# Second mixer of a two-layer trunk: the joins of the block inverses in four parts each, and operands of three post steps requested one step ahead

## Chip, cores, metric

One Trainium2 chip, one core. The metric is the time of one execution in device microseconds (us); lower is better. All data are float32.

## What is computed

Two layers of a streaming encoder run on 1104 tokens side by side: 16 learned tokens and 1024 prompt tokens of one request, and 64 tokens of another that brings its own state. Layer 0 is a gated delta-rule mixer with an MLP, layer 1 the mixer that the change is in (RWKV-7) with an MLP. Cut to layer 1's mixer, for the normalised input h (D = 1024, 16 heads of 64):

```python
xx = shift(h) - h
xr, xw, xk, xv, xa, xg = h + xx * mu          # six mixes
r, k, v = xr @ w_r, xk @ w_k, xv @ w_v
w_log = -softplus(-(w0 + tanh(xw @ w1) @ w2)) - 0.5
a     = sigmoid(a0 + (xa @ a1) @ a2)
gate  = sigmoid(xg @ g1) @ g2
kk = l2_normalize(k * k_k);  k = k * (1 + (a - 1) * k_a);  decay = exp(-exp(w_log))
# per head and token t
S = S * decay_t + (S @ -kk_t) (kk_t * a_t)^T + v_t k_t^T
y_t = S @ r_t
y = group_norm(y) * ln_w + ln_b + sum(r * k * r_k) * v
out = (y * gate) @ w_o
```

## The kernel before, in words

Activations lie with the features on the 128 partitions and tokens along the rows; tokens are worked on in three groups (336, 384, 384). Every large product is made in three TensorE products of two-part operands: a weight comes as a 512 KB `raw` tile, ScalarE (ACT) casts it to the high part `wh` (L108), VectorE (DVE) makes the low part `wl` (L109), and `mm3` (L125 to L131) multiplies. `wunit` (L111) requests `raw` and splits it in one go.

All loads and stores of the second mixer are issued by one queue, SyncE's (SP), in the order in which the program stands there. An engine does its instructions in order; where the next one waits, everything behind it on that engine waits too. The program is written as Python generators that `weave` (L570) mixes: of the generators that run side by side, the one that is furthest behind its weight takes the next step. The framework's scheduler then sets the final order on each engine, so an instruction can stand earlier or later than it was written.

The second mixer runs in these stages:

- `rwkv_a` (L1206): the products with w_r, the low-rank paths and w_k. `dense` (L1277) runs over feature blocks f = 0 to 7 and groups g = 0 to 2 and calls a post function for each of the 24 results. `post_k` (L1407) loads A (`l<-rA`) and the decays (`sw<-rSW`) and stores PQ, KR and BK. Their tiles have two buffers per tag.
- The product with w_v, with `post_v` (L1461): it loads `pq`, `kh` and `rt`, multiplies `rt` (L1468) and `kh` (L1470), makes a product over the heads (L1472), and stores V and, from the tile `pq`, BV. Two buffers per tag here too. Inside this stage the first block inverse is made, and at its end `gates` (L1153) loads the hidden gate values (`hx<-rHG`, nine loads, L1160), casts them (L1161) and starts the gate product (L1176).
- `rwkv_b` (L1644): six iterations i (three groups, two halves of the heads). In iteration i the state chain of i (`chain`), the operands of i+1 (`build`), the gram matrices of i+2 (`grams`), the inverse of i+1 (`inverse`, L1599) and the output of i-1 (`tail`, L1752) are woven. `tail` loads `lbv` and `lgt` for four feature blocks, normalises, and multiplies by w_o in four units, each with its own `wunit` (L1780); the pool `wp` holds two `raw` buffers and one `wh` and `wl` there.

`base_inverse` (L608) inverts 24 unit triangular blocks of 32x32 per partition quarter. DVE eliminates inside 16x16 blocks; the join of the two halves is two products of 96 small matrix products each (L630 and L639; the trace shows 192 TensorE instructions for either, beside as many weight loads). The result of the first is copied by ACT (L631), that of the second subtracted by DVE (L640). Each uses one PSUM tile of the tag B (`psB`), which has three buffers, shared with `build` and `grams`. The first mixer's inverses call the same function.

Of the kernel before, what the change touches and what calls it, by code (L numbers as in the profile page):

```python
# [16 lines left out]
P = 128  # L17
# [15 lines left out]
IN, D1, D2, GA = 24, 28, 10, 25  # L33
# [18 lines left out]
def tile_trunk(ctx, tc, *aps, stages=("gdn", "ffn0", "rwkv", "ffn1"), dbg=None):  # L52
# [7 lines left out]
    def uid(s):  # L60
        _n[0] += 1
        return f"{s}{_n[0]}"
# [48 lines left out]
    def wunit(src, p=None, eng=None):  # L111
        p = p or wp
        a = src.shape[1] if len(src.shape) == 3 else 1
        raw = p.tile([P, D], F32, tag="raw", bufs=rawb[0], name=uid("raw"))
        dst = raw.rearrange("p (a b) -> p a b", a=a) if a > 1 else raw
        nc.sync.dma_start(dst, src)
        h = p.tile([P, KT, P], F32R, tag="wh", name=uid("wh"))
        l = p.tile([P, KT, P], F32R, tag="wl", name=uid("wl"))
        split(h.rearrange("p a b -> p (a b)"), l.rearrange("p a b -> p (a b)"), raw, eng)
        return h, l  # L120
# [487 lines left out]
    def base_inverse(tp, d, beta, nb, tag, diag, evac, res, lag=1):  # L608
        a16, a = tile32(tp, "b32a")
        nc.vector.transpose(a, d.rearrange("p n i -> p i n"))  # L610
        if beta is not None:
            nc.vector.tensor_tensor(a, a, beta.unsqueeze(2).to_broadcast([P, 32, 32]), ALU.mult)
        t16, t = tile32(tp, "b32t")
        nc.gpsimd.memset(t, 0.0)
        nc.gpsimd.memset(t.rearrange("p i k -> p (i k)")[:, ::33], 1.0)
        yield from substitute(tp, a16, t16)
        tnh = tp.tile([P, 32, 16], F32, tag=tag, bufs=1, name=uid("b32tnh"))
        nc.vector.transpose(tnh.rearrange("p n k -> p k n"), t.rearrange("p i k -> p k i")[:, 0:16])
# [6 lines left out]
        ps = psB()  # L625
        pv = ps[:, :16 * nb].rearrange("p (n k) -> p n k", k=16)
        for n in range(nb):
            for b in range(4):
                r = slice(32 * b, 32 * b + 32)
                nc.tensor.matmul(pv[r, n], diag(b, n), tnh[r, n], start=True, stop=True)  # L630
        evac(v[:, 0:nb, 0:16], pv)  # L631
        for _ in range(lag):
            yield
        ps = psB()
        pv = ps[:, :16 * nb].rearrange("p (n k) -> p n k", k=16)
        for n in range(nb):
            for b in range(4):
                r = slice(32 * b, 32 * b + 32)
                nc.tensor.matmul(pv[r, n], v[r, n], tt[r, n, 16:32], start=True, stop=True)  # L639
        nc.vector.tensor_tensor(tt[:, 0:nb, 16:32], tt[:, 0:nb, 16:32], pv, ALU.subtract)  # L640
# [512 lines left out]
    def gates(tp, xp, dr):  # L1153
        w2 = ins["rwkv_g2"][0]
        hid = []
        for i in range(3):
            t = tp.tile([P, T], F32R, tag=f"hg{i}", bufs=1, name=uid("hg"))
            for c0, n in FULL:
                x = xp.tile([P, 384], F32, tag="ev", name=uid("hx"))
                nc.sync.dma_start(x[:, :n], dr["HG"][i, :, c0:c0 + n])  # L1160
                nc.scalar.copy(t[:, c0:c0 + n], x[:, :n])  # L1161
            yield
# [43 lines left out]
    def rwkv_a(hnp, col, prm, pc, plb, dr, esb, esx, esg, pend, esP):  # L1206
        C = math.exp(-0.5)
        with ExitStack() as es0, ExitStack() as es:
# [67 lines left out]

            def dense(s, w, post):  # L1277
# [5 lines left out]
                for fs in [(0, 1, 2), (3,), (4,), (5,), (6, 7)]:  # L1283
# [122 lines left out]

            def post_k(ps, n, g, f):  # L1407
                o = 384 - n
                A = load("l0", "A", f, g)
                sw = tmp("sw", [P, 390])  # L1410
                nc.sync.dma_start(sw, dr["SW"][f, :, 6 * g:6 * g + 6].rearrange("p a b -> p (a b)"))
# [43 lines left out]
            with ExitStack() as es, ExitStack() as es1:  # L1455
# [4 lines left out]

                def post_v(ps, n, g, f):  # L1461
                    o = 384 - n
                    cs = slice(g * 384, (g + 1) * 384)
                    pq, kh, rt = (mp.tile([P, 384], F32, tag=t, name=uid(t)) for t in ("pq", "kh", "rt"))
                    nc.sync.dma_start(pq, dr["PQ"][f, :, cs])
                    nc.sync.dma_start(kh, dr["BK"][1, f, :, cs])
                    nc.sync.dma_start(rt, dr["R"][f, :, cs])
# [19 lines left out]
                weave((4, d), (4, upto(4, gts)))  # L1487
# [17 lines left out]
    class batches:  # L1505
# [93 lines left out]
        def inverse(self, i):  # L1599
# [15 lines left out]
            yield from base_inverse(tp, dp, None, 24, "v1", diag, nc.scalar.copy, res, 2)  # L1615
# [28 lines left out]
    def rwkv_b(xT, rc, col, plb, dr, Bx, gts, esx, esg, esf, esh, F, more):  # L1644
# [9 lines left out]
        with ExitStack() as esw, ExitStack() as es, ExitStack() as est:  # L1654
# [97 lines left out]
            def tail(g, hf, B):  # L1752
                tp, lb, bd64 = tpt
                yy = [tp.tile([P, 4, 384], F32R, tag=t, bufs=1, name=uid(t)) for t in ("yh", "yl")]
# [24 lines left out]
                for mp in range(4):  # L1779
                    u = wunit(w_o[512 * hf:512 * hf + 512, 256 * mp:256 * mp + 256].rearrange("(k p) c -> p k c", p=P), *wpo)  # L1780
# [25 lines left out]
            for i, (g, hf) in enumerate(seq):  # L1806
# [33 lines left out]
                done = tail(g, hf, Bi)  # L1840
# [178 lines left out]
```

## Time and profile before

| | |
|---|---|
| time, median of 3 runs | 3339.27 us (3329.17 to 3344.31) |
| profiled execution: its own time | 3336.7 us |
| its span on the core | 3335.0 us |
| TensorE (PE) busy | 3154.0 us, 95% |
| VectorE (DVE), ScalarE (ACT) busy | 2420.6 us, 1552.3 us |
| w_v stage, from the start of its first weight load to the last L1472 | 1883.1 to 2048.5 us of the span |
| `rwkv_b`, iterations 0 to 4 | about 2060 to 2460 us |

A line such as `L310 PE MATMUL psA<-tc,sh` is line, engine, operation, result and operands; L numbers are lines of the kernel before. In rows of the timeline come the start in us, the duration in us, and in brackets how long the engine had stood idle and what released it. PEclk is the clock that was granted to TensorE, 1.00 being full.

### The profile page before, as it was taken

Reading aid. Unit: us, or ns where it says so; the run is one execution under the profiler, and the core shown is the slowest. Engines: PE = TensorE matmul, PEld = TensorE weight load, DVE = VectorE, ACT = ScalarE, POOL = GpSimd, SP = SyncE. Lnnn points to the kernel's source line nnn. Section 1 sums busy time; section 2 is a strip of 40 time slices with the busy share of each in tenths; the row PEclk is TensorE's granted clock in tenths of the full one; section 3 lists DMA queues with packets and bytes.
Section 4 is the critical chain, followed back from the end, with each engine's and each line's share of the span. In section 5 each row is a group of like instructions: output and inputs, shape, how many; then the busy total and the mean of one; then the engine's idle time right before and its main releaser. Section 6 shows DMA issues by size and latency. Waiting matters only on the chain. (4 is left out here: it accounts for less than half of the span.)

```text
span 3335.0 us, 72764 instructions
## 1 busy us (share of the span) xinstructions
PE 3154.0 (95%) x29154; PEld 2978.1 (89%) x29154; DVE 2420.6 (73%) x4836; ACT 1552.3 (47%) x3229; POOL 143.9 (4%) x236
## 2 busy tenths in 40 slices
PE   7999999898999999999999888889889999999998
PEld 7898988797999999999998777777778999999998
DVE  6867867557777667766978864777767687877775
ACT  5776866444433333212778733444445443333112
POOL 1000000002200000000001100000000310000000
PEclk9999999999999999999999999988889999999999
DMA  5443432884332225422255877555556332335231
GB/s 172 108 111 98 112 92 64 298 273 139 99 98 82 79 75 168 131 86 76 85 186 188 282 226 225 145 168 159 141 172 187 100 104 91 94 97 174 88 96 61
DMA packets 543924, 452.70 MB, mean 136 GB/s; under 512 B 78377, under 2 KB 494930, under 8 KB 543458
## 3 DMA queue, kind: packets, MB, share of 16 engines
q1 hardware_dynamic: 538682, 445.61, 43.5%
q8 instruction: 230, 3.77, 0.5%
q10 hardware_dynamic: 4904, 2.43, 0.3%
q14 instruction: 108, 0.88, 0.1%
HBM read 306.86 MB, written 141.07 MB: 134 GB/s over the span
## 5 line engine op out<-in xcount | busy, mean ns | idle before, releaser
L310 PE MATMUL psA<-tc,sh 128*128 128x276 f32 (+1 forms) x1712 | 499.7, 292 | 18.6 <-ACT sh L108 8.2
L312 PE MATMUL psA<-tc,sl 128*128 128x276 f32 (+1 forms) x1712 | 499.0, 291 | 4.0 <-DVE sl L109 3.9
L311 PE MATMUL psA<-tc,sh 128*128 128x276 f32 (+1 forms) x1712 | 498.9, 291 | 0.3 <-DVE tc L109 0.3
L406 DVE TENSOR_TENSOR xT<-xT,psA 128x384 f32<-128x384 f32 (+3 forms) x496 | 252.5, 520 | 136.0 <-PE psA L131 134.3
L310 PEld LDWEIGHTS psA<-tc,sh 128*128 128x128 f32 x1712 | 326.3, 191 | 21.3 <-ACT sh L108 8.6
L108 ACT CAST wh<-raw 128x1024 fp32r<-128x1024 f32 x159 | 166.2, 1048 | 370.6 <-PE psA L130 260.0
L312 PEld LDWEIGHTS psA<-tc,sl 128*128 128x128 f32 x1712 | 325.7, 190 | 5.0 <-DVE sl L109 4.7
L311 PEld LDWEIGHTS psA<-tc,sh 128*128 128x128 f32 x1712 | 326.0, 190 | 1.2 <-DVE tc L109 0.7
L129 PE MATMUL psA<-hh,wh 128*128 128x384 f32 (+3 forms) x1024 | 325.8, 320 | 1.2 <-ACT hh L108 1.2
L130 PE MATMUL psA<-hl,wh 128*128 128x384 f32 (+3 forms) x1024 | 326.4, 319 | 0.0
L131 PE MATMUL psA<-hh,wl 128*128 128x384 f32 (+3 forms) x1024 | 325.3, 318 | 0.0
L129 PE MATMUL psA<-hnh,wh 128*128 128x384 f32 (+1 forms) x768 | 263.9, 344 | 6.9 <-ACT hnh L108 4.1
L130 PE MATMUL psA<-hnl,wh 128*128 128x384 f32 (+1 forms) x768 | 264.8, 345 | 1.7 <-DVE hnl L109 1.7
L131 PE MATMUL psA<-hnh,wl 128*128 128x384 f32 (+1 forms) x768 | 264.2, 344 | 0.0
L109 DVE TENSOR_TENSOR wl<-raw,wh 128x1024 fp32r<-128x1024 f32 x159 | 195.1, 1229 | 74.5 <-ACT wh L108 73.8
L108 ACT CAST sh<-raw 128x512 fp32r<-128x512 f32 x202 | 124.2, 619 | 247.0 <-PE psA L311 219.3
L130 PE MATMUL psA<-mxl,wh 128*128 128x384 f32 (+1 forms) x672 | 228.2, 342 | 4.0 <-DVE mxl L109 3.7
L129 PE MATMUL psA<-mxh,wh 128*128 128x384 f32 (+1 forms) x672 | 224.5, 345 | 7.4 <-ACT wh L108 3.5
L131 PE MATMUL psA<-mxh,wl 128*128 128x384 f32 (+1 forms) x672 | 226.4, 339 | 0.4 <-DVE wl L109 0.4
L129 PEld LDWEIGHTS psA<-hh,wh 128*128 128x128 f32 x1024 | 192.1, 188 | 2.1 <-ACT hh L108 1.9
L130 PEld LDWEIGHTS psA<-hl,wh 128*128 128x128 f32 x1024 | 192.3, 188 | 0.3
L131 PEld LDWEIGHTS psA<-hh,wl 128*128 128x128 f32 x1024 | 192.5, 188 | 0.1
(493 smaller groups left out, 7944.3 us busy)
## 6 DMA issues: line engine op xcount, KB each, us to landing
raw<-in_ffn_w_gate_dram SPq DMA_DIRECT2D x64, 512.0 KB
raw<-in_ffn_w_up_dram SPq DMA_DIRECT2D x64, 512.0 KB
raw<-in_ffn_w_down_dram SPq DMA_DIRECT2D x44, 512.0 KB
raw<-in_gdn_w_in_dram SPq DMA_DIRECT2D x32, 512.0 KB
raw<-in_gdn_w_out_dram SPq DMA_DIRECT2D x24, 512.0 KB
raw<-in_rwkv_w_o_dram SPq DMA_DIRECT2D x24, 512.0 KB
hr<-dhid SPq DMA_DIRECT2D x44, 276.0 KB
hr<-dhid SPq DMA_DIRECT2D x44, 272.0 KB
```

What stands on the lines that cost most here:

```text
L108: nc.scalar.copy(h, src)
L109: (eng or nc.vector).tensor_tensor(l, src, h.bitcast(F32), ALU.subtract)
L129: nc.tensor.matmul(ps, w[0][:, k, :], x[0][:, k, :n], start=a, stop=False)
L130: nc.tensor.matmul(ps, w[0][:, k, :], x[1][:, k, :n], start=False, stop=False)
L131: nc.tensor.matmul(ps, w[1][:, k, :], x[0][:, k, :n], start=False, stop=z)
L310: nc.tensor.matmul(ps, u[0][:, kk], h, start=first and kk == 0, stop=False)
L311: nc.tensor.matmul(ps, u[0][:, kk], l, start=False, stop=False)
L312: nc.tensor.matmul(ps, u[1][:, kk], h, start=False, stop=last and kk == 3)
L406: nc.vector.tensor_tensor(xT[:, m, a:a + n], xT[:, m, a:a + n], pd[:, :n], ALU.add)
```

## The change

- `base_inverse` takes `parts`. The second mixer's inverses pass 4: each of the two joins is cut into four parts of 24 small products, each with a `psB` tile and an evacuation of its own (ACT 128x96, DVE 128x96), with a `yield` between parts. The first mixer's inverses pass nothing and stay as they were. The weights IN, D1 of `weave` go from 24 to 30 and from 28 to 35, since `inverse` has six more steps.
- `early` requests the operands of `post_k` and of `post_v` one call ahead of their use.
- `gates` loads each hidden row in two halves of 552 columns (six loads instead of nine), into one buffer of a tag of its own (`hx`), with a `yield` between a load and its cast.
- `wunit` is cut in `wraw` (the request) and `wsplit`. `tail` requests the first two w_o units at its start and each further one right after the split of the unit two before (depth 2); the tail of iteration 4 runs as before (depth 0).

```diff
-    def base_inverse(tp, d, beta, nb, tag, diag, evac, res, lag=1):
+    def base_inverse(tp, d, beta, nb, tag, diag, evac, res, lag=1, parts=1):
...
+        w = nb // parts
+        for a in range(0, nb, w):
+            if a:
+                yield
+            pv = psB()[:, :16 * w].rearrange("p (n k) -> p n k", k=16)
+            for n in range(w):
+                for b in range(4):
+                    r = slice(32 * b, 32 * b + 32)
+                    nc.tensor.matmul(pv[r, n], diag(b, a + n), tnh[r, a + n], start=True, stop=True)
+            evac(v[:, a:a + w, 0:16], pv)
...
-            for c0, n in FULL:
-                x = xp.tile([P, 384], F32, tag="ev", name=uid("hx"))
-                nc.sync.dma_start(x[:, :n], dr["HG"][i, :, c0:c0 + n])
-                nc.scalar.copy(t[:, c0:c0 + n], x[:, :n])
-            yield
+            for c in (slice(0, T // 2), slice(T // 2, T)):
+                x = xp.tile([P, T // 2], F32, tag="hx", bufs=1, name=uid("hx"))
+                nc.sync.dma_start(x, dr["HG"][i, :, c])
+                yield
+                nc.scalar.copy(t[:, c], x)
...
+            class early:
...
+                def take(self, g, f):
+                    self.fetch(self.order.index((g, f)) + 1)
+                    return self.got.pop((g, f))
...
-                A = load("l0", "A", f, g)
-                sw = tmp("sw", [P, 390])
-                nc.sync.dma_start(sw, dr["SW"][f, :, 6 * g:6 * g + 6].rearrange("p a b -> p (a b)"))
+                A, sw = asw.take(g, f)
...
-                    pq, kh, rt = (mp.tile([P, 384], F32, tag=t, name=uid(t)) for t in ("pq", "kh", "rt"))
...
+                    pq, kh, rt = pkr.take(g, f)
...
-            yield from base_inverse(tp, dp, None, 24, "v1", diag, nc.scalar.copy, res, 2)
+            yield from base_inverse(tp, dp, None, 24, "v1", diag, nc.scalar.copy, res, 2, 4)
...
-            def tail(g, hf, B):
+            def tail(g, hf, B, depth):
...
+                for mp in range(depth):
+                    fetch(mp)
...
-                    u = wunit(w_o[512 * hf:512 * hf + 512, 256 * mp:256 * mp + 256].rearrange("(k p) c -> p k c", p=P), *wpo)
+                    fetch(mp)
+                    u = wsplit(raws[mp], *wpo)
+                    if depth:
+                        fetch(mp + depth)
...
-                done = tail(g, hf, Bi)
+                done = tail(g, hf, Bi, 0 if i == 4 else 2)
```

What the change does to the order of instructions follows at three places (first the row of the kernel before, then of the changed one; the line numbers of the changed kernel are its own, and the numbers behind names count tiles).

TensorE, third inverse, during iteration 1: `b32tnh` and `at` are the operands of the first join, `b32tt` of the second, `W`, `kb`, `pm`, `ttf`, `xT` belong to the chain, `bk`, `rcx`, `V` to `build`, `gsq` to `tail`. Before:

```order
L1748 MATMUL psA_25176<-mb_24332,W_23793 64x64 x2
L1769 MATMUL psC_25423<-gsq_25264,bd_23240 128x320
L630 MATMUL psB_25320<-b32tnh_25232,at_23312 32x16 x96
L1586 MATMUL psB_25418<-ident,bk_25278 128x128
L1712 MATMUL psA_25305<-xT_14945 64x65
L1586 MATMUL psB_25418<-ident,bk_25278 128x128
L1712 MATMUL psA_25305<-xT_14945 64x65 x7
L1586 MATMUL psB_25418<-ident,bk_25278 128x128
L1722 MATMUL psA_25306<-xT_14945 64x64 x8
L1727 MATMUL psA_25440<-pm_25315,ttf_23209 64x65 x8
L1592 MATMUL psB_25451<-rcx,V_25279 64x65 x6
L639 MATMUL psB_25473<-b32tt_25234,b32t_25236 32x16 x2
```

After, the first two parts of the same join:

```order
L1774 MATMUL psA_25292<-W_23808,bt_23811 64x65
L1788 MATMUL psA_25210<-mb_23810,W_23808 64x64
L640 MATMUL psB_25257<-b32tnh_25203,at_23315 32x16 x24
L1632 MATMUL psB_25283<-rcx,V_25174 64x65 x6
L640 MATMUL psB_25305<-b32tnh_25203,at_23315 32x16 x24
L1615 MATMUL psB_25358<-kb_25346,bk_25349 64x64
L1617 MATMUL psB_25358<-kb_25346,bk_25349 64x128
L1615 MATMUL psB_25358<-kb_25346,bk_25349 64x64
L1615 MATMUL psB_25359<-kb_25346,bk_25349 64x64
L1617 MATMUL psB_25359<-kb_25346,bk_25349 64x128
```

and the last two, with the first rows of the second join:

```order
L640 MATMUL psB_25376<-b32tnh_25203,at_23315 32x16 x24
L1752 MATMUL psA_25402<-xT_14945 64x65
L1762 MATMUL psA_25403<-xT_14945 64x64
L1752 MATMUL psA_25402<-xT_14945 64x65 x7
L640 MATMUL psB_25417<-b32tnh_25203,at_23315 32x16 x24
L1626 MATMUL psB_25443<-ident,bk_25349 128x128 x3
L1818 MATMUL psC_25448<-gsq_25335,bd_23243 128x320
L1762 MATMUL psA_25403<-xT_14945 64x64 x7
L1767 MATMUL psA_25465<-pm_25412,ttf_23212 64x65 x8
L1632 MATMUL psB_25476<-rcx,V_25350 64x65 x6
L651 MATMUL psB_25498<-b32tt_25205,b32t_25207 32x16 x2
L1774 MATMUL psA_25485<-xT_14945 64x65
```

The 96 products of the first join stood in one row; now four parts of 24 stand with the chain's and the builder's products between them. In the first inverse, inside the w_v stage, the eight parts of both joins stand one behind the other with nothing between; four large products stood between its two joins before.

SyncE's queue, iteration 2, at the start of the tail of iteration 1 (`raw` is a w_o unit; `lbv`, `lgt` are the tail's other loads, `xt` and `dx` the residual, the rest belongs to `build` and `grams`). Before:

```order
L1566 DMA bk_26626<-rBK 64x3x64
L1569 DMA V_26500<-rV 128x192
L1566 DMA bk_26626<-rBK 64x3x64 x2
L1761 DMA lbv_26493<-rBV 128x320
L1566 DMA bk_26626<-rBK 64x3x64
L1763 DMA lgt_26495<-rGT 128x320
L1568 DMA xT_14945<-rKR 64x2x192 x2
L1540 DMA b_26919<-rBK 128x384
L1569 DMA V_26627<-rV 128x192
L1541 DMA k_26920<-rKR 128x384
L116 DMA raw_26937<-in_rwkv_w_o_dram 128x4x256
L1761 DMA lbv_26611<-rBV 128x320
```

After:

```order
L119 DMA raw_26277<-in_rwkv_w_o_dram 128x4x256
L1845 DMA dx<-xt_25971 128x320
L1810 DMA lbv_26283<-rBV 128x320
L1812 DMA lgt_26285<-rGT 128x320
L1810 DMA lbv_26376<-rBV 128x320
L1812 DMA lgt_26378<-rGT 128x320
L1608 DMA xT_14945<-rKR 64x2x192 x2
L1580 DMA b_26512<-rBK 128x384
L1845 DMA dx<-xt_26094 128x320
L1609 DMA V_26226<-rV 128x192
L1606 DMA bk_26382<-rBK 64x3x64 x2
L119 DMA raw_26279<-in_rwkv_w_o_dram 128x4x256
```

The tail's first w_o unit stood behind the loads of its third feature block; now two units stand at its start, the first ahead of all its other loads, 30 rows earlier in the queue.

ACT, end of the w_v stage (`hg<-hx` are the casts of the hidden gate values, `ev<-psA` the copies of w_v's last results, `go<-psC` the first gate results). Before:

```order
L1161 CAST hg_23035<-hx_23036 128x336
L1161 CAST hg_23035<-hx_23039 128x384
L1474 COPY ev_23081<-psA_23045 128x384
L1161 CAST hg_23035<-hx_23042 128x384
L1161 CAST hg_23086<-hx_23087 128x336
L1161 CAST hg_23086<-hx_23090 128x384
L1474 COPY ev_23132<-psA_23096 128x384
L1161 CAST hg_23086<-hx_23093 128x384
L1161 CAST hg_23137<-hx_23138 128x336
L1178 COPY go_23336<-psC_23331 128x320
L1161 CAST hg_23137<-hx_23141 128x384
L1474 COPY ev_23183<-psA_23147 128x384
```

After:

```order
L1174 CAST hg_23053<-hx_23057 128x552
L1514 COPY ev_23048<-psA_23012 128x384
L1174 CAST hg_23101<-hx_23102 128x552
L1514 COPY ev_23095<-psA_23059 128x384
L1174 CAST hg_23101<-hx_23105 128x552
L1514 COPY ev_23143<-psA_23107 128x384
L1174 CAST hg_23149<-hx_23150 128x552
L1514 COPY ev_23185<-psA_23155 128x384
L1174 CAST hg_23149<-hx_23153 128x552
L1190 COPY go_23339<-psC_23334 128x320
```

Two or three casts stood between two copies `ev`; now there is one, of 552 columns, and the first gate result is copied only behind the last cast.

More of the change, by code (lines that the diff above doesn't have):

```diff
@@ L32 @@
 CH, BU, GR, TA, LT = 36, 23, 4, 16, 12
-IN, D1, D2, GA = 24, 28, 10, 25
+IN, D1, D2, GA = 30, 35, 10, 25
 OP, HO, AH = 7, 2, 8
@@ L111, in wunit, with wraw @@
     def wunit(src, p=None, eng=None):
+        return wsplit(wraw(src, p), p, eng)
+    def wraw(src, p=None):
         p = p or wp
@@ L116, in wunit, with wsplit @@
         nc.sync.dma_start(dst, src)
+        return raw
+    def wsplit(raw, p=None, eng=None):
+        p = p or wp
         h = p.tile([P, KT, P], F32R, tag="wh", name=uid("wh"))
@@ L624, in base_inverse @@
             yield
[L625 to L631, printed above, removed]
+        w = nb // parts
[8 more added lines that the diff above has]
+            evac(v[:, a:a + w, 0:16], pv)
         for _ in range(lag):
             yield
[L634 to L640, printed above, removed]
+        for a in range(0, nb, w):
+            if a:
+                yield
+            pv = psB()[:, :16 * w].rearrange("p (n k) -> p n k", k=16)
+            for n in range(w):
+                for b in range(4):
+                    r = slice(32 * b, 32 * b + 32)
+                    nc.tensor.matmul(pv[r, n], v[r, a + n], tt[r, a + n, 16:32], start=True, stop=True)
+            nc.vector.tensor_tensor(tt[:, a:a + w, 16:32], tt[:, a:a + w, 16:32], pv, ALU.subtract)
         yield
@@ L1157, in gates @@
             t = tp.tile([P, T], F32R, tag=f"hg{i}", bufs=1, name=uid("hg"))
-            for c0, n in FULL:
-                x = xp.tile([P, 384], F32, tag="ev", name=uid("hx"))
-                nc.sync.dma_start(x[:, :n], dr["HG"][i, :, c0:c0 + n])
-                nc.scalar.copy(t[:, c0:c0 + n], x[:, :n])
-            yield
+            for c in (slice(0, T // 2), slice(T // 2, T)):
+                x = xp.tile([P, T // 2], F32, tag="hx", bufs=1, name=uid("hx"))
+                nc.sync.dma_start(x, dr["HG"][i, :, c])
+                yield
+                nc.scalar.copy(t[:, c], x)
             hid.append(t)
@@ L1275, in store, with __init__, fetch @@
                     nc.sync.dma_start(dr[name][f, :, g * 384:(g + 1) * 384], e)
+            FS = [(0, 1, 2), (3,), (4,), (5,), (6, 7)]
+            class early:
+                def __init__(self, load):
+                    self.load, self.got = load, {}
+                    self.order = [(g, f) for fs in FS for g in range(3) for f in fs]
+                    self.fetch(0)
+                def fetch(self, i):
+                    if i < len(self.order):
+                        self.got[self.order[i]] = self.load(*self.order[i])
+                def take(self, g, f):
+                    self.fetch(self.order.index((g, f)) + 1)
+                    return self.got.pop((g, f))
             def dense(s, w, post):
@@ L1281, in prep @@
                     m[g] = mix(s, g, (mp if g else mp0, f"mx{g}", 0))
-                for fs in [(0, 1, 2), (3,), (4,), (5,), (6, 7)]:
+                for fs in FS:
                     us = [colunit(w, f * P) for f in fs]
@@ L1405, in c3, with load_asw @@
                 return t.rearrange("p (c t) -> p c t", t=64)
+            def load_asw(g, f):
+                sw = tmp("sw", [P, 390])
+                nc.sync.dma_start(sw, dr["SW"][f, :, 6 * g:6 * g + 6].rearrange("p a b -> p (a b)"))
+                return load("l0", "A", f, g), sw
+            asw = early(load_asw)
             def post_k(ps, n, g, f):
                 o = 384 - n
-                A = load("l0", "A", f, g)
-                sw = tmp("sw", [P, 390])
-                nc.sync.dma_start(sw, dr["SW"][f, :, 6 * g:6 * g + 6].rearrange("p a b -> p (a b)"))
+                A, sw = asw.take(g, f)
                 sq = tmp("sq")
@@ L1459, in rwkv_a, with load_pkr @@
                 mp0 = pool(es1, "rm0", 2)
+                def load_pkr(g, f):
+                    cs = slice(g * 384, (g + 1) * 384)
+                    pq, kh, rt = (mp.tile([P, 384], F32, tag=t, name=uid(t)) for t in ("pq", "kh", "rt"))
+                    nc.sync.dma_start(pq, dr["PQ"][f, :, cs])
+                    nc.sync.dma_start(rt, dr["R"][f, :, cs])
+                    nc.sync.dma_start(kh, dr["BK"][1, f, :, cs])
+                    return pq, kh, rt
+                pkr = early(load_pkr)
                 def post_v(ps, n, g, f):
@@ L1463, in post_v @@
                     cs = slice(g * 384, (g + 1) * 384)
-                    pq, kh, rt = (mp.tile([P, 384], F32, tag=t, name=uid(t)) for t in ("pq", "kh", "rt"))
-                    nc.sync.dma_start(pq, dr["PQ"][f, :, cs])
-                    nc.sync.dma_start(kh, dr["BK"][1, f, :, cs])
-                    nc.sync.dma_start(rt, dr["R"][f, :, cs])
+                    pq, kh, rt = pkr.take(g, f)
                     nc.vector.tensor_tensor(rt, rt, pq, ALU.mult)
@@ L1486, in rwkv_a @@
                 gts = gates(pool(esg, "rg", 2, side="right"), mp, dr)
-                weave((4, d), (4, upto(4, gts)))
+                weave((4, d), (7, upto(7, gts)))
             return Bx, gts
@@ L1750, in chain, with fetch @@
                     yield
-            def tail(g, hf, B):
+            def tail(g, hf, B, depth):
                 tp, lb, bd64 = tpt
+                raws = []
+                def fetch(mp):
+                    if mp < 4 and mp == len(raws):
+                        raws.append(wraw(w_o[512 * hf:512 * hf + 512, 256 * mp:256 * mp + 256]
+                                         .rearrange("(k p) c -> p k c", p=P), *wpo))
+                for mp in range(depth):
+                    fetch(mp)
                 yy = [tp.tile([P, 4, 384], F32R, tag=t, bufs=1, name=uid(t)) for t in ("yh", "yl")]
```

## Prediction

> **What bounds the kernel now.** The page comes first, to see whether TensorE stands still anywhere and at what clock it runs.
>
> ```profile
> span 3335.0 us, 72764 instructions
> ...
> PEclk9999999999999999999999999988889999999999
> ...
> q8 instruction: 230, 3.77, 0.5%
> ```
>
> Each slice is 83.4 us. TensorE is busy nearly everywhere, so a wait of another engine costs only what TensorE then stands still. The clock is below 0.9 in slices 27 to 30 (2168 to 2502 us), inside `rwkv_b`. The order moves instructions only from the w_k pass to iteration 4 (about 1740 to 2560 us), and the whole gain or loss must come from there. The next view is the list of TensorE's waits (engine, line, releaser: us in total, times, longest) in iterations 0 to 4, and one row of ACT's.
>
> ```profile
> PE psB L630 <- issue: 9.0, 3, 3.4
> PE psA L1734 <- ACT W L1728: 6.8, 4, 5.6
> PE psB L639 <- issue: 4.1, 3, 1.9
> PE psA L1712 <- DVE xT L1740: 3.1, 4, 1.7
> ...
> PE psA L1734 <- DVE xT L1729: 2.2, 1, 2.2
> ...
> PE psB L1575 <- ACT W L1596: 0.6, 2, 0.4
> ```
>
> ```profile
> ACT wh L108 <- DMA raw<-in_rwkv_w_o_dram: 14.1, 3, 7.2
> ```
>
> The two largest items are those that the change aims at: 13.1 us in which TensorE waits "for nothing that the profile shows" inside the joins, and 5.6 us in which the chain waits for an ACT copy. The timeline says why ACT is late.
>
> ```profile
> 2240.50 0.38 SPq L116 DMA_DIRECT2D raw<-in_rwkv_w_o_dram  x1
> ...
> 2244.81 1.04 ACT L108 CAST wh<-raw 128x1024 fp32r<-128x1024 f32 x1 [5.45 <-DMA raw<-in_rwkv_w_o_dram]
> ...
> 2246.61 0.48 PE L1734 MATMUL psA<-W,bt 128*64 128x65 f32 x2 [5.61 <-ACT W L1728]
> ```
>
> ```profile
> 2305.43 0.27 PE L1575 MATMUL psB<-kb,bk 64*64 64x64 f32 x1 [1.88 <-ACT bt L1587]
> ```
>
> ACT stood 5.45 us at the cast of a w_o unit whose request had left only 4.3 us before; the copy of `W` was behind the cast, the chain behind the copy. The second case, at 2304, goes the same way (ACT waits 7.2 us) and costs TensorE 1.88. Then the clock. Each row is a stretch: its length, the busy time of PE, PEld, DVE, ACT and POOL, then the granted clock, the DMA share and GB/s. The first is the start of the w_v stage, the others lie in `rwkv_b`.
>
> ```profile
> 1884.00:1897.00 13.00, 7.04 (x21) 5.19 (x22) 10.39 (x20) 8.21 (x15) 4.45 (x11) 0.61 1.00 314
> ...
> 2101.00:2108.00 7.00, 4.23 (x156) 3.77 (x146) 3.05 (x7) 1.28 (x3) 0.42 (x1) 0.77 0.46 128
> 2174.00:2190.00 16.00, 14.21 (x345) 12.31 (x345) 8.07 (x16) 4.80 (x10) 1.11 (x2) 0.50 0.39 111
> ...
> 2253.00:2272.00 19.00, 18.49 (x522) 16.46 (x525) 11.05 (x23) 5.83 (x12) 1.53 (x3) 0.50 0.41 117
> 2303.00:2312.00 9.00, 7.12 (x119) 5.56 (x115) 5.46 (x15) 4.58 (x10) 0.00 (x0) 0.81 0.45 120
> 2329.00:2354.00 25.00, 20.36 (x525) 17.34 (x526) 15.32 (x31) 7.41 (x15) 1.53 (x3) 0.52 0.44 117
> 2410.00:2434.00 24.00, 19.73 (x556) 16.85 (x552) 16.93 (x36) 7.64 (x16) 0.85 (x4) 0.64 0.21 54
> ```
>
> ```profile
> 2246.00:2253.00 7.00, 4.90 (x48) 3.38 (x48) 6.79 (x14) 2.75 (x8) 0.00 (x0) 0.50 0.69 200
> ```
>
> The clock is halved in and around every join from the third inverse on. What that costs is seen in one kind of product, at full clock (2192 to 2240 us) and then at half (2253 to 2272 us):
>
> ```profile
> L131 PE MATMUL psC<-yh,wl 128*128 128x320 f32 x28 | 8.6, 313 | 0.1
> ```
>
> ```profile
> L131 PE MATMUL psC<-yh,wl 128*128 128x320 f32 x4 | 1.9, 468 | 0.0
> ```
>
> 468 against 313 ns: of busy time at half clock a third (1 - 313/468 = 0.33) would be saved at full clock.
>
> **The change part by part.** All sums are made against the profiled execution, 3336.7 us, which lies 2.6 us below the median of the runs.
>
> T1, first w_o unit of a tail. In the order both units stand at the tail's start, the first 30 rows earlier on SP. At 2245 the wait of 5.6 us goes. What is late next is the chain's own waits for DVE (2.2 and 1.7 us in the list). The clock: stretches 2246 to 2253 and 2253 to 2272 hold 4.90 + 18.49 = 23.4 us of busy time at half clock, which began with this wait: 0.33 x 23.4 = 7.7 us at most, nothing if the join in it halves the clock by itself. I take 5, since the wait stands just ahead. T1 = -5.6 - 5.0 = -10.6, ends 0 and -13.3.
>
> [...]
>
> T2, the unit at 2304. Units 2 and 3 are requested right after an earlier split. The 1.88 us go; at 0.81 of the clock over 9 us, 3.4 us ran at half: 0.33 x 3.4 = 1.1. T2 = -3.0, ends 0 and -3.0.
>
> T3, the hidden gate values. Rows from the list of waits in the w_v stage, then two from the timeline:
>
> ```profile
> DVE rt L1468 <- DMA pq<-rPQ: 29.0, 12, 5.6
> ```
>
> ```profile
> PE psC L1176 <- ACT hg L1161: 2.2, 2, 1.4
> ...
> PE psC L1176 <- ACT go L1178: 1.1, 2, 0.6
> ```
>
> ```profile
> 2041.29 0.91 PE L1472 MATMUL psC<-kh,bd 128*128 128x384 f32 x2 [0.85 <-DVE kh L1470]
> ...
> 2047.63 0.91 PE L1472 MATMUL psC<-kh,bd 128*128 128x384 f32 x2 [1.26 <-DVE kh L1470]
> ```
>
> In the changed order every cast of `hx` stands ahead of the first gate result, and six loads are spread over the last posts. The gate's waits go: 2.2 + 1.1 = -3.3. The waits for `kh` hang on `pq`; if the shorter queue frees them too, -2.1 more; if one buffer makes each load wait for the cast before it, nothing is gained. T3 = -3.3, ends 0 and -5.4.
>
> T4, the five inverses in `rwkv_b`. The stalls have a period. Below, the second join of the first inverse, then the first join of the third:
>
> ```profile
> 1959.59 1.90 PE L639 MATMUL psB<-b32tt,b32t 32*32 32x16 f32 x128 [2.38 <-issue]
> ...
> 1964.98 0.55 PE L639 MATMUL psB<-b32tt,b32t 32*32 32x16 f32 x25 [3.49 <-issue]
> ```
>
> ```profile
> 2170.19 1.71 PE L630 MATMUL psB<-b32tnh,at 32*32 32x16 f32 x150 [0.18 <-DVE b32tnh L618]
> ...
> 2175.32 0.77 PE L630 MATMUL psB<-b32tnh,at 32*32 32x16 f32 x42 [3.42 <-issue]
> ```
>
> Between two stalls lie 128 products with 128 weight loads, 256 instructions in 5.4 us (1959.59 to 1964.98), while a join issues 150 products with their loads in 1.71 us: it uses instructions up faster than they come. In the changed order parts of 96 instructions alternate with other products. The first 300 instructions of a join, used in 1.7 us before, then last about 3.0, so each of the three stalls of a first join loses about 1.3 us: -3.9. Before the second joins more lies between, and I take their two long stalls, 3.8 of the 4.1 us, as gone. That is -7.7, ends 0 and -13.1. The clock: the stretches at 2101 (0.23 x 7 x 2 = 3.2 us at half) and 2174 (14.21 us) begin with such a stall, 0.33 x 17.4 = 5.8 us, of which I take half, -2.9. Those at 2329 and 2410 are at half clock for 8 to 10 us ahead of their stalls:
>
> ```profile
> 2330.00:2338.00 8.00, 7.07 (x196) 5.27 (x193) 7.80 (x15) 2.28 (x5) 0.42 (x1) 0.51 0.87 225
> 2412.00:2422.00 10.00, 8.82 (x253) 7.20 (x255) 7.41 (x14) 3.46 (x7) 0.85 (x4) 0.50 0.30 77
> ```
>
> There waits of the chain come first, and I take 0 for them, with 0.33 x (20.36 + 14.2) = 11.4 us as the end (14.2 is 0.72 of 19.73 us, the part at half clock).
>
> Against this stands the price of the parts. The rows are groups by shape in iterations 0 to 4 (busy us, mean ns):
>
> ```profile
> L109 DVE TENSOR_TENSOR wl<-raw,wh 128x1024 fp32r<-128x1024 f32 x15 | 18.3, 1223 | 8.7 <-ACT wh L108 8.6
> ...
> L640 DVE TENSOR_TENSOR b32tt<-b32tt,psB 128x384 f32<-128x384 f32 x5 | 2.8, 555 | 6.4 <-PE psB L639 6.3
> ...
> L602 DVE TENSOR_TENSOR b32u<-b32a,b32t 128x96 f32<-128x96 f32 x10 | 2.6, 257 | 0.3
> ...
> L631 ACT COPY b32t<-psB 128x384 f32<-128x384 f32 x5 | 2.4, 479 | 13.0 <-PE psB L630 13.0
> ```
>
> DVE's four evacuations of 96 columns cost 4 x 257 - 555 = 473 ns more per inverse, ACT's about as much: 4.8 us over five inverses on engines that wait often; I take +1 (0 to +4.8). The parts also take `psB` tiles, 8 instead of 2 per inverse, 30 more in five. With three buffers TensorE waits when a copy is late. Nearest is L1575, which waited 0.3 us each time for a copy of such a tile; I take that for half of the 30, +4.5 (0 to +42, below). T4 = -7.7 - 2.9 + 1 + 4.5 = -5.1.
>
> T5, the first inverse: its parts stand one behind the other, so nothing fills the stalls: 0 (-2 to +2).
>
> T6, from w_k to w_v. SP now has `pq`, `kh` and `rt` of the first post ahead of the first two w_v units.
>
> ```profile
> 1888.82 0.65 PE L129 MATMUL psA<-mxh,wh 128*128 128x336 f32 x1 [3.50 <-ACT wh L108]
> ```
>
> TensorE already waits 3.5 us for the first cast there, and DMA is full (1.00, 314 GB/s, first stretch above). Three tiles of 128x384 are 0.59 MB, 1.9 us at that rate, and their issues some 1 us: +2.5 (0 to +4).
>
> T7, the requests one call ahead: on SP `pq` of the next post still stands behind the store of the last (two buffers), and `rt` before `kh` is all that moves; the 29.0 us of DVE's wait stay: 0 (-2 to +3).
>
> Sum: -10.6 - 3.0 - 3.3 - 5.1 + 0 + 2.5 + 0 = -19.5, 3317.2 beside the profiled 3336.7, and 3319.8 in the median's terms. About 0.5% (17 us) is what a measurement of this kernel can tell from no change.
>
> **The rivals.** A: the parts bring nothing. If the stalls come by the count of instructions alone, they fall at other places and stay as long. T4 is then +5.5, the sum -10.6 - 3.0 - 3.3 + 5.5 + 2.5 = -8.9: 3330.4. For it: the period holds to the instruction; against it: a stall is shorter where other work lies between (1.9 us in later second joins, 3.49 here). [...]
>
> B: without a long wait the clock never falls in these iterations. T1 -13.3, T2 -3.0, T3 -5.4, T4 -13.1 - 5.8 - 11.4 + 1 = -29.3, T6 +2.5: -48.5, 3290.8. For it: the clock is 1.00 between the joins. Against it: the two stretches above fall before any stall, and the change doesn't touch the chain's own waits.
>
> C, slower: TensorE waits for `psB` at each part, because its evacuation stands behind a cast or split of w_o. Price: DVE 1.22 + 0.26 = 1.48, ACT 1.04 + about 0.24 = 1.3, mean 1.4; 30 x 1.4 = 42 in place of 4.5: +18, 3357.3. It decides from (19.5 + 4.5) / 30 = 0.8 us per tile, where the gain is gone. For it: the first evacuation of a join now stands among work that was behind it. Against it: the order leaves other products between most parts, and the waits for copies are small now.
>
> That the requests of T7 do nothing is in the forecast already.
>
> **How the numbers follow.** Forecast 0.48, A 0.26, B 0.14, C 0.12. Faster by over 0.5%: 0.30 of the forecast's, 0.14 of B, 0.04 of A, 0.48. Within: 0.18, 0.20 of A, 0.06 of C, 0.44. Slower: 0.06 of C and 0.02 of the forecast's bad ends, 0.08. The range 3293 to 3346 leaves out half of B and half of C, and some bad ends.
>
> **What would show it.** Right: no wait of ACT for `raw` of w_o at 2240 to 2310 and L1734's 5.6 gone; the waits "issue" at the joins down from 13.1 to about 5; gate waits gone; the wait ahead of w_v's first product longer, about 6; `rt`'s 29 us unchanged; the clock at 1.00 over most of the stretches at 2246 and 2174. Wrong: waits for `psB` copies at the joins of over 10 us, stalls that sum to 13 again, or half clock over longer stretches than before.

## The result, and the profile after

The changed kernel takes 3317.55 us in the median of 6 runs (3312.32 to 3323.71), the kernel before 3337.89 us (6 runs beside it). The ratio is 0.9941, 95% interval 0.9928 to 0.9953: 20.3 us less, where 19.5 were forecast. Its profiled execution took 3312.32 us. First the page after: span and granted clock.

```profile
span 3310.4 us, 72805 instructions
...
PEclk9999999999999999999999999989899999999999
```

The four slices below 0.9 have become two. Next TensorE's waits in the iterations 0 to 4 (2060 to 2460 us), in the order of the list; line numbers are the changed kernel's: L640 and L651 are the two joins, L641 the copy of a part, L1774 the chain's product that was L1734, L1752 the one that was L1712.

```profile
PE psA L1752 <- DVE W L1780: 8.1, 5, 3.3
PE psA L1774 <- ACT W L1768: 3.3, 5, 1.4
...
PE psB L640 <- ACT b32t L641: 0.7, 1, 0.7
...
PE psB L651 <- issue: 0.5, 1, 0.5
...
PE psB L1615 <- ACT b32t L641: 0.4, 1, 0.4
```

The joins stood 13.1 us for "issue" before and stand 0.5 now. The 5.6 us behind the w_o unit are gone (the longest wait of that product for `W` is 1.4), and no cast of a w_o unit waits for its transfer any more. The new `psB` tiles cost 1.1 us of waits. The largest wait is now the chain's own for DVE: what was late next. The stretches of the iterations 2, 3 and 4 in the kernel before, and then in the changed one (length, busy PE, PEld, DVE, ACT, POOL, then clock, DMA share, GB/s):

```profile
2221.00:2302.00 81.00, 71.55 (x1572) 60.74 (x1570) 59.52 (x138) 35.80 (x79) 1.84 (x4) 0.83 0.59 169
2302.00:2388.00 86.00, 75.17 (x1570) 63.66 (x1568) 62.12 (x143) 36.71 (x80) 1.84 (x4) 0.84 0.52 146
2388.00:2466.00 78.00, 70.13 (x1504) 58.91 (x1503) 56.03 (x124) 32.84 (x74) 0.85 (x4) 0.89 0.45 132
```

```profile
2220.00:2292.00 72.00, 66.67 (x1571) 56.62 (x1572) 59.21 (x140) 35.87 (x83) 1.85 (x4) 0.95 0.61 173
2292.00:2366.00 74.00, 70.06 (x1567) 58.94 (x1566) 61.76 (x143) 36.09 (x83) 1.85 (x4) 0.95 0.59 168
2366.00:2440.00 74.00, 68.85 (x1502) 57.76 (x1502) 56.79 (x131) 32.85 (x76) 0.85 (x4) 0.91 0.50 146
```

The counts of products agree, so each pair of rows holds the same work: 9, 12 and 4 us less, about as much as the whole span lost (24.6 us). TensorE's busy time fell too (75.17 to 70.06 in iteration 3): the same products ran at a higher clock (0.95 in place of 0.84). Ahead of the iterations things went back and forth. In the w_v stage and at its end:

```profile
DVE rt L1508 <- DMA pq<-rPQ: 25.4, 10, 8.0
...
ACT hg L1174 <- DMA hx<-rHG: 15.8, 5, 3.7
```

```profile
2056.68 0.33 PE L1615 MATMUL psB<-kb,bk 64*64 64x64 f32 x1 [3.74 <-DMA kb<-rKR]
```

DVE waits for `pq` almost as long as before (29.0). The casts of `hx` wait nearly as long as before (15.8 against 17.0), but the gate product no longer waits for them. In its place TensorE waits 3.74 us for `kb`, a load of the builder, a little later.

### The profile page after: what moved, and what is told of

Read it like the earlier page. It is cut to its first block, busy times and chain, and to the rows that moved or that the text cites. A ratio compares the mean times of both kernels' runs of the same rounds, so it can differ in the third digit from the quotient of the medians.

```text
span 3310.4 us, 72805 instructions
## 1 busy us (share of the span) xinstructions
PE 3145.6 (95%) x29154; PEld 2968.5 (90%) x29154; DVE 2423.5 (73%) x4854; ACT 1552.8 (47%) x3244; POOL 145.1 (4%) x236
```

## Experiments

All ratios are to the kernel before, which ran beside each group of experiments on the same chip (its medians there were 3345 to 3347 us). The groups ran on four chips: `p_only`, `p_block`, `w_only`, `rest` on one, `pw`, `wr`, `pr`, `after2` on another, `ord`, `seam`, `parts8` on a third, `parts2` on a fourth. A profile is one execution of its kernel.

**The parts alone, the parts without spreading, the w_o units alone, the rest alone.** `p_only` keeps the parts and their weights and undoes the other pieces:

```diff
-                done = tail(g, hf, Bi, 0 if i == 4 else 2)
+                done = tail(g, hf, Bi, 0)
...
-                    self.fetch(self.order.index((g, f)) + 1)
+                    self.fetch(self.order.index((g, f)))
```

with `gates` as before. 

> Only the parts: both joins in four parts with the new weights of the weave; w_o units, hidden gate values and operands of the posts requested as before. If a join stalls because it uses instructions up faster than they arrive, the waits named issue at the two joins in rwkv_b fall from 13.1 us to under 2 and half-clock stretches end inside the joins: 8 to 18 us faster than before, while ACT still waits over 5 us for a w_o unit. If the parts bring nothing (stalls by count alone), the stalls still sum to about 13 us and the time is 2 to 8 us longer than before.

`p_block` is the same with the `yield` between parts taken out and IN, D1 at 24, 28:

```diff
             for a in range(0, nb, w):
-                if a:
-                    yield
                 pv = psB()[:, :16 * w].rearrange("p (n k) -> p n k", k=16)
```

> The same four parts with their own PSUM tiles and copies, but written without a step between them and with the old weights, so that the parts of a join stand nearly one behind the other; all else as before. If it is the spreading that helps, the stalls at the joins stay at 9 us or more and the time is within 5 us of before, on either side. If it is the smaller tiles and earlier copies that help, it gains as much as the kernel with the parts alone. If the PSUM tiles are the price (rival C), PE waits for the copies ACT b32t and DVE b32tt by over 10 us here and the time is 10 us or more longer.

`w_only` undoes the parts (`parts` 1, IN, D1 at 24, 28), the gates and the requests one ahead, and keeps `depth` 2. 

> Only the w_o units requested ahead; joins whole, hidden gate values and operands of the posts as before. By the terms T1 and T2 the waits of 5.6 and 1.9 us go and the clock stays up ahead of the third and fourth joins: 9 to 14 us faster than before. If the joins halve the clock by themselves, only the waits go: 5 to 8 us faster, and the stretch of half clock around the join after 2245 stays over 15 us long. The stalls at the joins stay at 10 us or more by both.

`rest` undoes the parts and the w_o units (depth 0) and keeps gates and requests. 

> Only the hidden gate values in halves and the operands of the posts one call ahead; joins whole, w_o units as before. By the terms T3, T6 and T7 (-3.3, +2.5, 0): within 4 us of before, with the gate product's waits gone and a longer wait ahead of w_v's first product. If the requests one call ahead do hide DVE's wait for pq, that wait falls from 29 to under 15 us and the time by 5 us or more.

Measured: `p_only` 0.9989 (0.9978 to 1.0001), `p_block` 1.0050 (1.0034 to 1.0067), `w_only` 0.9999 (0.9988 to 1.0010), `rest` 0.9992 (0.9977 to 1.0007). Taken as they stand, no piece is worth anything by itself, and most expectations were missed: `p_only` was to gain 8 to 18 us and gained 4, `w_only` at least 5 and gained nothing, `p_block` was to stay within 5 us of before and was 17 us slower; only `rest` came out as expected. Yet the profile of `p_only` has what its first expectation named, joins that wait no more than 1.0 us in all for "issue" (no row for the first one):

```profile
PE psB L651 <- issue: 1.0, 1, 1.0
```

And `p_block`, with the same tiles and copies but the parts nearly in a row, has the stalls:

```profile
PE psB L647 <- issue: 6.2, 4, 2.0
PE psB L638 <- issue: 3.5, 2, 1.9
...
PE psB L638 <- ACT b32t L639: 1.4, 1, 1.4
```

9.7 us, against 1.0; 1.0050 / 0.9989 = 1.0061, some 20 us between the two. So it is the spreading (the `yield`s with the new weights of the weave; what the weights do alone was not run) that takes the stalls away, not the smaller tiles or the earlier copies, and waits for `psB` copies (1.4 us here) are no large price. `p_only` shows a second thing: with the joins out of the way TensorE runs into a late w_o unit in iteration 2 for longer than before (8.45 against 5.61 us).

```profile
2257.11 0.38 SPq L119 DMA_DIRECT2D raw<-in_rwkv_w_o_dram  x1
2262.49 1.04 ACT L108 CAST wh<-raw 128x1024 fp32r<-128x1024 f32 x1 [8.23 <-DMA raw<-in_rwkv_w_o_dram]
...
2264.97 1.44 PE L1817 MATMUL psC<-gsq,bd 128*128 128x320 f32 x2 [8.45 <-ACT gsq L1814]
```

I formed a theory from this: parts and early units need each other.

**Pairs, and the changed kernel again.** `pw` is the changed kernel with gates and requests undone as in `p_only`; `wr` has `parts` 1 and the old weights; `pr` has depth 0.

```diff
-            yield from base_inverse(tp, dp, None, 24, "v1", diag, nc.scalar.copy, res, 2, 4)
+            yield from base_inverse(tp, dp, None, 24, "v1", diag, nc.scalar.copy, res, 2)
```

> Parts and early w_o units together, hidden gate values and operands of the posts as before. Theory of the pair: with the parts alone TensorE comes to the tail sooner and stands 8.5 us for a late w_o unit, and with early units alone the joins still stall and halve the clock; only together do both waits go. Then the time is 10 to 18 us below before (ratio 0.9946 to 0.997), with half-clock time in rwkv_b near 60 us against about 110. If the gains simply add, it is 0.9989 x 0.9999, some 4 us below before.

> The changed kernel with whole joins (the rest of the change kept). By the theory of the pair the parts are needed: within 6 us of before, stalls at the joins of 9 us or more. If the interaction lies between the early w_o units and the gate values and post operands (they share SP's queue), it is 10 us or more below before.

> The changed kernel with w_o units requested as before (the rest of the change kept). By the theory of the pair the early units are needed: 2 to 9 us below before, with a wait of 5 us or more behind a w_o unit. If the parts need only the gate values and post operands, it is 12 us or more below before.

> The changed kernel once more, for its ratio on the same chip as its pieces: 0.9935 to 0.9955 of before, if the gain does not depend on the chip. If the pieces came out small only since that chip differs, this comes out near 0.998 as well.

Measured: `pw` 0.9954 (0.9936 to 0.9972), `wr` 0.9965 (0.9949 to 0.9981), `pr` 0.9950 (0.9934 to 0.9966), `after2` 0.9919 (0.9903 to 0.9934). The pair gave what the theory asked for, but so did two pairs that it had no room for: `wr` lies 12 us below before although it has no parts, `pr` 17 us without the early units. The theory falls. `after2`, too, lies outside the 0.9935 to 0.9955 that were expected: the same kernel came out at 0.9941 first and at 0.9919 here, a difference just beyond the two intervals, of which the cause is not known. Four kernels, `p_only`, `p_block`, `w_only` and `pw`, have something else in common: they undo the requests one ahead at the call, but keep the order of the loads in it. In all four the w_v stage was longer, 169 to 176 us by the profile against 163 to 166 in the kernel before, the changed one, `after2`, `rest` and `wr`. (`pr`, with 169, and later `seam`, with 173, don't fit this sign, so it needed a run of its own.)

**The order of the loads alone.** `ord` undoes all pieces of the change in that way, so it is the kernel before but for the order of loads in `post_k` and `post_v`:

```diff
-                A = load("l0", "A", f, g)
-                sw = tmp("sw", [P, 390])
-                nc.sync.dma_start(sw, dr["SW"][f, :, 6 * g:6 * g + 6].rearrange("p a b -> p (a b)"))
+                sw = tmp("sw", [P, 390])
+                nc.sync.dma_start(sw, dr["SW"][f, :, 6 * g:6 * g + 6].rearrange("p a b -> p (a b)"))
+                A = load("l0", "A", f, g)
...
-                    nc.sync.dma_start(kh, dr["BK"][1, f, :, cs])
                     nc.sync.dma_start(rt, dr["R"][f, :, cs])
+                    nc.sync.dma_start(kh, dr["BK"][1, f, :, cs])
```

> None of the three parts of the change, but the order of the loads that four earlier runs (p_only, p_block, w_only, pw) had in the posts: sw ahead of A, rt ahead of kh, at the call itself. In those four the stage from w_v's first unit to its last product over the heads took 169 to 176 us in the profile, 165 to 166 in the kernels that have the loads as the kernel before or the changed one has them. If that order of loads costs the 5 to 8 us, this is 0.1 to 0.35% slower than before, the stage is 169 us or longer, and the four runs must be read against this one: parts and early w_o units then are worth 0.3% or so each and add up. If the order of loads costs nothing, this is within 0.1% of before and the gains truly need each other.

Measured: 1.0030 (1.0015 to 1.0044). The first alternative holds. The w_v stage in `ord`, and in it the stretch from the first inverse on; below, the same stage in the kernel before:

```profile
1884.00:2062.00 178.00, 153.31 (x1458) 131.36 (x1460) 105.44 (x203) 69.53 (x137) 12.11 (x26) 0.88 0.76 234
1964.00:1986.00 22.00, 18.70 (x435) 14.77 (x434) 5.91 (x11) 5.56 (x9) 1.11 (x2) 0.53 0.41 119
```

```profile
1883.00:2048.00 165.00, 141.88 (x1453) 123.51 (x1454) 101.08 (x196) 66.42 (x132) 10.64 (x24) 0.94 0.80 244
```

TensorE stands still hardly longer (24.7 against 23.1 us, length less busy time); busy time is 11 us longer for the same products, at 0.88 of the clock instead of 0.94. So `p_only`, `p_block`, `w_only` and `pw` are read against `ord`:

| | ratio to | value |
|---|---|---|
| parts | `p_only` / `ord` | 0.9989 / 1.0030 = 0.9959 |
| parts | `after2` / `wr` | 0.9919 / 0.9965 = 0.9954 |
| early w_o units | `w_only` / `ord` | 0.9999 / 1.0030 = 0.9969 |
| early w_o units | `after2` / `pr` | 0.9919 / 0.9950 = 0.9969 |
| both | `pw` / `ord` | 0.9954 / 1.0030 = 0.9924 |
| rest | `rest` | 0.9992 |
| parts not spread | `p_block` / `ord` | 1.0050 / 1.0030 = 1.0020 |

Each ratio of two is uncertain by about 0.002 (both half intervals, added in squares). Those to `wr` and `pr` are between runs on one chip; those to `ord` go across chips, which may add as much as the two measurements of the changed kernel differ by (0.9941 and 0.9919). Within that the pieces add: 0.41 to 0.46% for the parts, 0.31% for the units, 0.08% for the rest, 0.8 to 0.85% in all, and `after2` has 0.81%. A piece has the same worth, within the noise, whether it is added first or last. Read against `ord`, `p_only` (14 us) and `w_only` (10 us) lie where their first expectations put them (8 to 18 and 9 to 14). Parts that aren't spread (1.0020) gain nothing and may cost some.

**Two variations.** `seam` requests the operands of w_v's first post at its call:

```diff
-                pkr = early(load_pkr)
+                pkr = early(load_pkr, False)
```

(False leaves out the first `fetch`). 

> The changed kernel, but the operands of w_v's first post are requested at its call and not ahead of w_v's first units. By T6 the w_v units come some 2 to 3 us sooner, TensorE's wait ahead of w_v's first product falls by 2 us or more against the changed kernel, and the time by 1 to 3 us (a ratio to before lower by up to 0.001). If the first post then waits for its operands as long, nothing is gained.

 Measured: 0.9935 (0.9914 to 0.9956), between the two measurements of the changed kernel (0.9941 and 0.9919), so the time shows neither a gain nor a loss. The start of the w_v stage in the changed kernel, then in `seam`:

```profile
1889.61 1.65 PE L1512 MATMUL psC<-kh,bd 128*128 128x384 f32 x2 [5.72 <-DVE kh L1510]
...
1890.05 1.05 ACT L108 CAST wh<-raw 128x1024 fp32r<-128x1024 f32 x1 [4.68 <-DMA raw<-in_rwkv_w_v_dram]
...
1893.91 0.93 PE L136 MATMUL psA<-mxh,wh 128*128 128x336 f32 x2 [2.66 <-ACT mxh L108]
```

```profile
1891.74 1.04 ACT L108 CAST wh<-raw 128x1024 fp32r<-128x1024 f32 x1 [0.85 <-DMA raw<-in_rwkv_w_v_dram]
1894.89 1.04 ACT L108 CAST wh<-raw 128x1024 fp32r<-128x1024 f32 x1 [2.11 <-DMA raw<-in_rwkv_w_v_dram]
...
1896.36 0.93 PE L136 MATMUL psA<-mxh,wh 128*128 128x336 f32 x2 [6.97 <-ACT mxh L108]
```

ACT's wait for the first unit fell from 4.68 to 0.85 us, as T6 has it. In the changed kernel the first post's product over the heads (L1512), whose operands are there early, stands on TensorE ahead of the first w_v product: TensorE waits 5.72 us for it and then 2.66 more, in `seam` 6.97 in one piece. In both kernels the first w_v product waits for the cast of the activations `mxh`, which stands on ACT behind the casts of two units, and the second unit came 2.11 us late in `seam`. From the end of w_k's last product to the start of w_v's first lie 6.5 us in the kernel before, 11.6 in the changed one and 8.6 in `seam`: some 3 us came back. The whole stage was longer in `seam` all the same, 172.9 us by the profile against 162.9, 5.5 us of that TensorE's busy time; why is not known.

`parts2` and `parts8` have 2 and 8 in place of 4, IN and D1 at 26, 30 and 38, 44:

```diff
-            yield from base_inverse(tp, dp, None, 24, "v1", diag, nc.scalar.copy, res, 2, 4)
+            yield from base_inverse(tp, dp, None, 24, "v1", diag, nc.scalar.copy, res, 2, 8)
```

> The changed kernel with the joins in eight parts and the weights of the weave raised in step. If the gain comes from spreading and four parts leave something, the half-clock time in rwkv_b falls below 58 us and the time by 3 us or more against the changed kernel. If four parts already take the stalls away, it is the same or up to 10 us slower, by 80 more small copies of 200 to 260 ns and as many PSUM tiles.

> The changed kernel with the joins in two parts (weights of the weave between), the middle of the row whole (0.9965 of before), four parts (0.9919), eight parts (0.9962). If spreading is bought with small copies and PSUM tiles, two parts take part of both: 0.993 to 0.9955, with stalls named issue at the joins of 3 to 8 us and half-clock stretches that end between the two parts or after them. If what counts is that a part is shorter than the distance of two stalls (two parts of 192 instructions are), two parts do as well as four or better: 0.992 or less, stalls under 2 us.

Measured: `parts8` 0.9962 (0.9947 to 0.9977), `parts2` 0.9950 (0.9932 to 0.9969). Whole joins have 0.9965 (`wr`), four parts 0.9919 and, measured first, 0.9941: four parts have the lowest ratio, but these runs are from different chips, and against 0.9941 neither two parts nor eight are worse by more than the intervals. `parts8`, some 14 us above `after2`, is beyond the 10 us that were expected at most; `parts2` has the time of its first expectation with fewer stalls than it named (3 to 8 us). Waits at the joins in two parts (iterations 0 to 4), and in eight:

```profile
PE psB L651 <- issue: 2.2, 2, 1.2
```

```profile
PE psB L640 <- ACT bt L1627: 1.7, 3, 0.6
...
PE psB L651 <- DVE kb L1621: 1.2, 5, 0.3
```

Two parts still stall a little (2.2 us, with 192 instructions a part). Eight don't, but join products wait eight times for a `psB` tile that the builder's copies hold, 2.9 us in these rows. So waits for `psB`, the cost that rival C names, appear at twice the tiles, though behind the builder's copies and not behind a cast or split of w_o. They are not the whole: the iterations 2 to 4 take 75.0, 77.6 and 78.1 us by the profile against 72.5, 73.4 and 74.3 in `after2`, 10.5 us more, with 5.5 us more idle time of TensorE. Where the rest of it lies was not settled. No version was clearly faster than the changed kernel.

## Why the prediction was right, point by point

The total was right (20.3 us, 19.5 forecast), and so were the mechanisms of the two large terms. That it fits to 1 us is partly luck: beside the pieces, in `after2`, the change was worth 27 us (0.81%), and there the terms don't fit each by itself. T1 and T2 were to give 13.6 us and gave about 10, T4 5.1 and gave 14 to 15.

There is a slip in the prediction's chances: by rival their parts come to 0.50 for the forecast (0.30, 0.18, 0.02) and 0.24 for A (0.04, 0.20), where 0.48 and 0.26 are given.

The table shows where the profiles have their time. Lengths run from the last w_o product of one iteration to that of the next (iteration 1 from the last gate product), read from the timeline; half clock is 2 x (1 - granted clock), summed over windows of 2 us in iterations 1 to 4.

| us | it. 1 | it. 2 | it. 3 | it. 4 | half clock |
|---|---|---|---|---|---|
| before | 82.2 | 80.8 | 86.0 | 78.3 | 92 |
| `ord` | 86.7 | 81.1 | 82.2 | 77.8 | 85 |
| `w_only` | 84.0 | 74.8 | 79.3 | 77.8 | 65 |
| `p_only` | 91.5 | 82.9 | 75.7 | 74.4 | 82 |
| `p_block` | 81.7 | 82.8 | 85.5 | 78.1 | 89 |
| `rest` | 84.5 | 80.6 | 85.2 | 78.3 | 92 |
| `wr` | 83.7 | 74.2 | 81.2 | 75.8 | 55 |
| `pr` | 87.8 | 82.7 | 79.9 | 72.1 | 68 |
| `pw` | 91.5 | 74.4 | 74.6 | 74.4 | 61 |
| changed | 85.2 | 71.9 | 74.1 | 74.2 | 48 |
| `after2` | 81.5 | 72.5 | 73.4 | 74.3 | 34 |

A profile is one execution, and the gain of a piece does not lie at the same place in every pair: the parts have 13.2 us in these four iterations between `wr` and `after2`, but 3.3 between `ord` and `p_only`, where iteration 1 became longer and the rest lies ahead of it (w_v stage 178.0 to 172.8 us, iteration 0, from there to the last gate product, 92.3 to 88.0).

- T1 and T2, the w_o units (-10.6 and -3.0): the waits went as said. The units are worth 0.31%, 10 us of the 13.6. `w_only` against `ord` has 6.3 us in iteration 2 and 2.9 in iteration 3, T2's 3.0. In iteration 2 the 6.3 us are 3.2 of idle time (the 5.7 us wait of `ord` went, but other waits came, the largest 2.3 us "issue" at a gram product) and 3.1 of busy time, the clock part. With the parts beside them they are more: 8.5 us between `p_only` and `pw` (4.0 of them busy time), 10.2 between `pr` and `after2` (4.2). So T1's clock part of 5 us was somewhat too large, and its wait of 5.6 us was not gained whole where joins are whole. Its mechanism is borne out: half clock in iteration 2 is 20.5 to 30.7 us in the six kernels with late units (before, `ord`, `p_only`, `p_block`, `rest`, `pr`) and 3.4 to 13.7 us in those with early ones (`w_only`, `wr`, `pw`, changed, `after2`).
- T3, the gate (-3.3): the gate's waits went, but the builder's load of `kb` is late next (3.74 us, quoted above). The term named no wait behind the gate's.
- T4, the five inverses (-5.1): the term that was furthest off. The parts are worth 0.41 to 0.46%, 14 to 15 us. The stalls were to lose 7.7 and lost 12.6 (13.1 to 0.5); the `psB` waits were to cost 4.5 and cost 1.1. And the step that failed is the clock: I took 0 for the stretches at 2329 and 2410, "at half clock before their stalls". They did begin with the chain's waits in the changed kernel too, but the first ended sooner:

```profile
2311.00:2315.00 4.00, 3.53 (x46) 2.74 (x44) 3.78 (x12) 1.76 (x4) 0.00 (x0) 0.57 0.78 216
2318.00:2322.00 4.00, 4.00 (x98) 3.25 (x94) 2.97 (x8) 0.97 (x4) 0.00 (x0) 0.58 0.37 88
2322.00:2338.00 16.00, 15.85 (x468) 13.87 (x468) 12.58 (x30) 6.60 (x17) 0.46 (x1) 1.00 0.53 155
```

 Two stretches of half clock of 3.4 us each, and then full clock through the rest of both joins, in place of 24 us at half. `p_block` in iteration 3, with the parts in a row, takes 85.5 us, as before. That the spread parts shorten half-clock stretches is shown for iteration 3: 20.5 to 27.3 us at half in the six kernels with whole joins or parts in a row (before, `ord`, `w_only`, `p_block`, `rest`, `wr`), 3.4 to 13.7 with four spread parts (`p_only`, `pw`, `pr`, changed, `after2`). In iteration 4 the two groups overlap (10.2 to 20.5 against 3.4 to 13.7). And it isn't a rule: the clock that was to be at 1.00 in the place of the stretch at 2174 stayed at half for 13.7 us in the changed kernel (17.1 before; 3.4 in `after2`), and in `p_only`, iteration 1, the clock stayed at half with TensorE busy throughout and the parts spread:

```profile
2185.00:2206.00 21.00, 20.49 (x380) 17.09 (x383) 12.05 (x28) 7.02 (x19) 0.42 (x1) 0.51 0.45 121
```

 What brings the clock back is open.
- T5, the first inverse (0), as forecast: its parts stand in a row, and it stalls still (4.6 us named "issue" at its second join, 5.9 before).
- T6 (+2.5): right in kind and too small at its place. The first w_v product started at 1893.91 against 1888.82, 5 us later, while w_k's last products started within 0.1 us of each other. It was given back inside the stage, which ended at 2047.8 against 2048.5 us, and undoing it in `seam` brought no gain that shows in the time. T7 (0): the requests one ahead hid nothing of `pq`'s wait (25.4 against 29.0). T3, T5, T6 and T7 together were -0.8; `rest` measured -0.08%, 2.7 us, with an interval that holds 0.
- Rival A is refuted by `p_only` against `p_block`: spread parts stall for 1 us, parts in a row for 9.7. Whole joins stalled for 13.1 us in the kernel before, 12.7 in `ord` and 8.1 in `wr`, in five inverses each. That it is instructions that TensorE waits for was not shown; it is argued from the count, and the count is strict: the seven stalls of over 0.9 us at the second mixer's joins in the kernel before lie 256, 3328, 512, 2560, 6400 and 3584 TensorE instructions (products, weight loads and the semaphore instructions among them) apart, each a multiple of 256 whatever stands between (counted in the trace); the two that are left in the changed kernel, 2.49 and 2.12 us in the first inverse, lie 256 apart.
- Rival B went too far (27 us at most, 48.5 asked); half clock still follows waits of the chain itself (2.04 us at 2308, 3.12 us at 2381 in the changed kernel). Rival C is not seen with four parts (1.1 us of waits for `psB`); with eight such waits appear.

The lengths of half clock have a unit: in the iterations of the kernel before, the changed one, `after2`, `ord`, `w_only` and `p_only` the stretches last 3.4, 6.8, 10.2, 13.7, 17.1, 20.5, 23.9 or 27.3 us, multiples of 3.4. What sets the clock to half and keeps it there is not shown: the stretch at 2311 in the changed kernel begins after a wait of 2.04 us, and the stretch of 20 us in `p_only` stayed at half with TensorE busy 20.49 of 21 us by the profile.

## What to carry to other kernels

Look for stalls named "issue" in bursts of very short products. Here they took 13.1 us in five inverses, came at multiples of 256 instructions, and fell to 0.5 us when the burst was cut into parts of 96 instructions that alternate with longer work (parts of 192: 2.2 us; parts of 96 in a row: 9.7 us). That the burst waits there for its own instructions is an estimate from that count. Cut as far as the stalls go and no further: each part takes an accumulator tile and a copy, and eight parts gained nothing over four (0.9962 against 0.9919 and 0.9941). And where an experiment undoes one piece of a change, undo it to the letter, or run the undone kernel itself: the order of four loads here moved the time by 0.30%, as much as the pieces that were to be measured (0.31% and 0.41 to 0.46%).

## What was not expected of the hardware

The order of loads in the posts (`ord`) costs 0.30% although TensorE's idle time in the w_v stage hardly moves (24.7 against 23.1 us): the stage had 44 us of half clock in place of 20 (summed over windows as in the table above). Why the order of loads moves the clock is open. In the kernel before, a wait of 1.88 us at 2304 was followed by 3.4 us at half clock and one of 2.20 us at 2327 by 23.9 us, at a price of a third of the busy time (313 against 468 ns for one kind of product). Waits alone don't tell the time of these kernels: the changed kernel's iteration 1 took 81.5 us in one profile and 85.2 in another (10.2 and 20.5 us of half clock).
